# A two-layer transformer with attention and 32 experts on one core: the host lays out every input

## The chip, the cores and the metric

The kernel runs on one core of one Trainium2 chip. The metric is the device time of one execution in microseconds (us), as a median of runs. The engines are TensorE (PE, matrix products; PEld loads its weights), VectorE (DVE), ScalarE (ACT), GpSimd (POOL) and SyncE (SP), which here only issues DMAs. TensorE's clock has two levels, 1.2 and 2.4 GHz; the profile gives the granted clock as a share of the higher one. What the host does with the inputs before the launch is outside the metric.

## The reference

256 tokens with 1024 features go through two layers. Layer 0 has NSA attention (three branches: compressed blocks of keys, selected blocks, a window), layer 1 MoBA attention with keys of its own. After each attention come a mixture of experts (group softmax, then the two best of 8 experts in the token's group) and a gate on a per-layer embedding p. Cut to what matters:

```
for l in (0, 1):
    xn = rms_norm(h, ln_mix[l])
    h  = h + attention_l(xn)                # w_in / w_q, compress_blocks(w1, w2), w_out
    xn = rms_norm(h, ln_ffn[l])
    cw = route(xn @ w_group + b_group, xn @ w_expert + b_expert)        # two experts per token
    h  = h + sum_e cw[:, e] * ((silu(xn @ w_gate[e]) * (xn @ w_up[e])) @ w_down[e])
    h  = h + sigmoid(rms_norm(h, ln_ple[l]) @ ple_w_gate[l]) * (p[l] @ ple_w_proj[l])
```

All inputs and the output are float32; each expert has 1024 x 128, 1024 x 128 and 128 x 1024 weights.

## The kernel before

The residual h stands in SBUF with the token on the partition (two tiles of 128 tokens x 1024 features). A feature product needs the feature on the partition, so `Transposed.fill` (L310) turns h with PE, four 128 x 128 transposes into PSUM, and `split` (L370) cuts the result into a high part (a cast on ACT) and a rest (a subtraction on DVE); three matmuls (L381 to L383: high x high, rest x high or high x rest, and the third) then stand for one product in full precision.

Weights come in through `load`, DMAs on SP's queue into a ring of buffers. `Weights` loads a 1024 x 512 matrix as four tiles of two blocks of 128 rows each (`raw`); `prep` multiplies each block by the norm's gain and splits it: ACT writes the high part (L145), DVE the rest (L146). Where heads are to stand in pairs (`paired`), the high part is L139 and the rest two half operations (L142). `chain` preps three blocks ahead of the one that PE works on. The gains are the columns `g_mix`, made from rows of the norm vectors by a PE transpose (L183) at the start; the other small vectors take a second one (L238).

The head, in its order on PE: L183, 16 transposes of x (L310), four matmuls on ones that compute nothing (`keep_warm`, L177), then the product with the compressed keys' and values' weights (B_c), whose result DVE scales (L331), copies (L651, L652) and adds to positions (L660), then the product with the first selected-branch weights (B_s0), then 32 matmuls with w1 (L702) over which the head norm's matmul L341 is spread.

In attention, `Embedding.turn` (L603 to L608) turns p with four PE transposes and an ACT copy, and L613 uses the result. L485 to L503 turn the softmax's probabilities and multiply them by the values; L472 is a softmax scale on POOL.

The experts of a layer run in eight groups j of four, each with room for 32 tokens, and a ninth short pass for one crowded expert. Before them stands the routing, per half t of the tokens: `logits`, `choose` (DVE, L960 to L970), `order` (PE, L985; DVE, L986) and `place` (DVE, L976), which writes the 0/1 matrix that `gather_first` (PE, L1017) multiplies with h. For that, h is split once more into `h_hi` and `h_lo`: `split_h` on ACT (L995), `rest_h` on DVE (L998). Both read h through `columns(t)` (L289), a view "(p k) -> k p": the feature p*8 + k belongs to block k, so neighbours in a block stand 8 words apart in h. During the experts `unsplit_h` (DVE, L1003) joins the parts to h again through the same view. The four gathers of 128 tokens per group pair alternate between DVE (L1090) and ACT (L1088) after PE's L1064. An expert's gate and up weights come by two DMAs of 512 KB (`load_wgu`, L879 to L888) into one tile; for j = 0 and j = 3 these are large named tiles, of which the fourth (XH in layer 0, XA in layer 1) is the one that holds h, so that its load can be issued only after L998 of the second half has read h.

The order of work on each engine is set by a scheduler that places instructions by their due times when the kernel is built; `tc.issue_after` adds constraints. A DMA on SP can't start before the tile that it writes is free.

## Time and profile before

| | |
|---|---|
| median of 3 runs | 552.87 us (551.81 to 553.31) |
| profiled execution, its own time | 552.15 us |
| its span, first to last instruction | 550.5 us |
| mean granted clock of TensorE | 0.990 |
| PE busy / DVE busy / ACT busy | 523.7 / 351.9 / 282.8 us |
| DMA | 146.14 MB, mean 265 GB/s |

The profiled execution is 0.72 us under the median, and 1.65 us of it lie outside the span. The busy time of an engine overlaps that of the others; what sets the end is read from the waits of the engine that is nearly always busy, and from the instructions around each of them.

### The profile page before, as it was taken

The numbers are of one execution on the slowest core, as the hardware profiler recorded it, in microseconds if no ns is written. First come the engines' busy times: TensorE is split into PE (matmuls) and PEld (weight loads), VectorE is DVE, ScalarE is ACT, GpSimd is POOL, SyncE is SP. The second block draws the span as 40 slices with busy tenths as digits, with TensorE's granted clock in tenths as the row PEclk, the third lists the DMA queues.
The fourth block names the chain that finished last, engine by engine and source line by source line (L and its number), as shares of the span: only waits on it lengthen the run. The fifth ranks groups of instructions, "written<-read, shape, count | busy, mean of one in ns | idle before, by whom it ended". The sixth has DMA issues, their size and how long they took to land. (4 is left out here: it accounts for less than half of the span.)

```text
span 550.5 us, 10449 instructions
## 1 busy us (share of the span) xinstructions
PE 523.7 (95%) x3804; PEld 373.5 (68%) x3804; DVE 351.9 (64%) x1072; ACT 282.8 (51%) x652; POOL 57.9 (11%) x128
## 2 busy tenths in 40 slices
PE   6999999999897999999999999999987999999996
PEld 6979996677567765464568999656556755555376
DVE  5869979988757645323278986767657535232484
ACT  6759468975526142222379956754352412222391
POOL 5000614213320003100000000000000013000000
PEclk9999999999999899999999999999998999999999
DMA  8986980255778499999972679944672999999702
GB/s 324 356 323 223 189 206 1 86 190 205 299 241 302 176 417 408 391 402 409 387 244 78 208 192 216 405 160 199 224 265 106 402 411 413 410 408 395 272 2 77
DMA packets 52940, 146.14 MB, mean 265 GB/s; under 512 B 5293, under 2 KB 10277, under 8 KB 52885
## 3 DMA queue, kind: packets, MB, share of 16 engines
q1 hardware_dynamic: 51669, 143.38, 72.4%
q0 software_dynamic: 1184, 2.05, 1.4%
q8 instruction: 31, 0.51, 0.4%
q14 instruction: 24, 0.20, 0.1%
q10 hardware_dynamic: 32, 0.01, 0.0%
HBM read 145.94 MB, written 1.05 MB: 267 GB/s over the span
## 5 line engine op out<-in xcount | busy, mean ns | idle before, releaser
L1225 PE MATMUL pb<-wgu,X 128*32 128x256 f32 x768 | 50.4, 380 | 1.0 <-DVE sinf L1150 0.4
L461 ACT ACTIVATE p<-p,mx 128x128 f32<-128x128 f32 (+1 forms) x96 | 42.5, 446 | 9.4 <-DVE mx L459 9.4
L865 ACT ACTIVATE p<-pb,srs 128x128 f32<-128x128 f32 x16 | 5.9, 368 | 80.5 <-PE pb L1225 71.0
L1225 PEld LDWEIGHTS pb<-wgu,X 128*32 128x32 f32 x768 | 29.7, 110 | 17.7 <-issue 2.2
L1270 PE MATMUL pb<-wd,hT 128*32 128x512 f32 x224 | 41.4, 596 | 0.0
L370 DVE TENSOR_TENSOR pta<-pb,p 128x512 fp32r<-128x512 f32 (+1 forms) x36 | 24.8, 690 | 24.0 <-ACT p L370 22.5
L370 ACT CAST p<-pb 128x512 fp32r<-128x512 f32 (+1 forms) x36 | 21.1, 585 | 34.7 <-PE pb L1270 33.2
L381 PE MATMUL pa<-XA,wsp 128*128 128x256 f32 x128 | 37.4, 292 | 0.0
L382 PE MATMUL pa<-XB,wsp 128*128 128x256 f32 x128 | 36.3, 284 | 0.0
L383 PE MATMUL pa<-XA,wsp 128*128 128x256 f32 x128 | 35.9, 282 | 0.0
L868 DVE TENSOR_TENSOR p<-pb,ptb 128x128 f32<-128x128 f32 (+1 forms) x18 | 5.2, 290 | 44.1 <-ACT ptb L867 41.8
L459 DVE CUSTOM_DVE_ANT_0 p<-pb,d_q 128x128 f32<-128x128 f32 (+1 forms) x96 | 29.6, 350 | 4.5 <-PE pb L442 3.4
L490 ACT COPY pta<-pa 128x512 f32<-128x512 f32 (+1 forms) x32 | 14.6, 478 | 34.0 <-PE pa L486 33.8
L472 POOL TENSOR_SCALAR p<-p,cf 128x128 f32<-128x128 f32 x32 | 24.8, 783 | 62.8 <-ACT p L461 29.0
L146 DVE SCALAR_TENSOR_TENSOR wsp<-raw,cols,wsp 128x512 fp32r<-128x512 f32 x40 | 28.0, 747 | 3.4 <-ACT wsp L145 3.3
L571 PE MATMUL pa<-wo,XH 128*128 128x512 f32 x64 | 29.4, 602 | 0.0
L1064 PE MATMUL pb<-rs,X 128*128 128x256 f32 (+1 forms) x192 | 27.1, 293 | 2.0 <-DVE X L1090 2.0
L1064 PEld LDWEIGHTS pb<-rs,X 128*128 128x128 f32 x192 | 24.3, 188 | 5.7 <-DVE X L1090 2.6
L1263 PE MATMUL pa<-p,rrow 128*128 128x512 f32 (+1 forms) x72 | 27.3, 424 | 0.0
L1263 PE MATMUL pa<-pta,rrow 128*128 128x512 f32 (+1 forms) x72 | 26.7, 420 | 0.4 <-DVE pta L370 0.4
L142 DVE SCALAR_TENSOR_TENSOR wsp<-raw,g_mix,wsp 128x256 fp32r<-128x256 f32 x64 | 26.5, 475 | 0.0
L145 ACT ACTIVATE wsp<-raw,cols 128x512 fp32r<-128x512 f32 x40 | 26.2, 717 | 0.0
(385 smaller groups left out, 1464.9 us busy)
## 6 DMA issues: line engine op xcount, KB each, us to landing
wgu<-in_moe_w_gate_dram SPq DMA_DIRECT2D x48, 512.0 KB, 6.5
wgu<-in_moe_w_up_dram SPq DMA_DIRECT2D x48, 512.0 KB, 10.2
wd<-in_moe_w_down_dram SPq DMA_DIRECT2D x48, 512.0 KB, 8.8
raw<-in_a_w_in_dram SPq DMA_DIRECT2D x16, 512.0 KB, 6.0
raw<-in_ple_w_gate_dram SPq DMA_DIRECT2D x16, 512.0 KB, 8.3
wd<-in_moe_w_down_dram SPq DMA_DIRECT2D x16, 256.0 KB, 6.2
wo<-in_a_w_out_dram SPq DMA_DIRECT2D x8, 512.0 KB, 8.4
raw<-in_b_w_q_dram SPq DMA_DIRECT2D x8, 512.0 KB, 4.4
```

What stands on the lines that cost most here:

```text
L146: nc.vector.scalar_tensor_tensor(lo, src, g, hi.bitcast(F32), ALU.mult, ALU.subtract)
L370: return nc.scalar.copy(hi, src), eng.tensor_tensor(lo, src, hi.bitcast(F32), ALU.subtract)
L381: nc.tensor.matmul(o, a[0], b[0], start=first, stop=False)
L382: nc.tensor.matmul(o, a[0], b[1], start=False, stop=False)
L383: return nc.tensor.matmul(o, a[1], b[0], start=False, stop=last)
L459: nc.vector.tensor_tensor_reduce(pt_[:, br, :], st_[:, br, :], dt_, -SLOPE[hh], 3e38, ALU.add, ALU.min, accum_out=mx[:, t, br:br + 1])
L461: mark["exp", c] = nc.scalar.activation(pt_[:, br, :], pt_[:, br, :], AF.Exp, bias=mx[:, t, br:br + 1], scale=-1.0, accum_out=sums[:, t, b ...
L571: m = nc.tensor.matmul(pt, self.oT[0][:, 2 * j + i, t * P:(t + 1) * P], self.raw[j][:, i, n * 512:(n + 1) * 512], start=(i == 0), stop=(i ...
L1064: nc.tensor.matmul(pt, part_columns(x, t)[:, k, :], Gs[i][:, t, 0:e1], start=(t == x == 0), stop=(t == x == 1))
L1225: last_ = nc.tensor.matmul(gu[32 * i:32 * i + 32, 0:2], xg[:, k, 32 * i:32 * i + 32], wgu[i][k], start=(k == 0), stop=(k == NK - 1), tile_ ...
L1263: nc.tensor.matmul(y[t][n], gt[0:m, t * P:(t + 1) * P], ysx[x][0:m], start=(first and x == 0), stop=(final and x == 1))
L1270: nc.tensor.matmul(ysp[32 * i:32 * i + 32, :], hT[:, 32 * i:32 * i + 32], wd[i][n], start=True, stop=True, tile_position=(0, 32 * i))
```

## The change

The host hands the inputs over in the shape in which SBUF holds them. (1) x comes also turned (`xT`); `cut` splits it straight from SBUF, interleaved with B_c's preps, and the 16 transposes go. x itself is loaded behind B_c's weights, 1 MB more in all. (2) All norm vectors and positions come as one table of columns, `vec`, by one DMA on ACT's queue with 312 bytes per partition; ten small DMAs, two PE transposes and their copies go. (3) `keep_warm` runs eight matmuls at PE's very start. (4) p comes turned; `turn` goes. (5) Projection weights lie in blocks, in pairs of heads where that is wanted: one contiguous run per partition in each DMA (4 KB instead of two of 2 KB; w1 16 KB instead of 16 runs of 1 KB; w_out, gate and up 8 KB), and one L131 in place of two L142. (6) Gate and up of one expert come by one DMA of 1 MB. (7) The experts' weights, the router and its gain stand in h's own order, "(k p)", so that a block of h is 128 neighbouring words. (8) The fourth tile of j = 0 moves to the ring; the late one is now used by j = 1. Line numbers below are those of the kernel after.

```diff
-                self.raw.append(load([P, 2, self.n], lambda t: [(t, wrows(w, c0, c1)[:, k:k + 2])], "raw"))
-                if small:
-                    nc.sync.dma_start(*small.pop(0))
+                if turned is not None:
+                    xT.append(load([P, 2, S], lambda t: [(t, turned[:, k:k + 2])], "xT"))
+                self.raw.append(load([P, 2, self.n], lambda t: [(t, w[:, k:k + 2])], "raw"))
...
-                    for b in range(2):
-                        o = pairs(lo)[:, :, b, :]
-                        nc.vector.scalar_tensor_tensor(o, src[:, b * 256:(b + 1) * 256].rearrange("p (i d) -> p i d", d=HD),
-                                                       g, pairs(hi)[:, :, b, :].bitcast(F32), ALU.mult, ALU.subtract)
+                nc.scalar.activation(hi, src, AF.Copy, scale=g)
+                nc.vector.scalar_tensor_tensor(lo, src, g, hi.bitcast(F32), ALU.mult, ALU.subtract)
...
+    vec = cp.tile([P, 78], F32, name="vec")
+    nc.scalar.dma_start(vec, I["vec"])
+    g_mix = vec[:, 0:16].rearrange("p (l k) -> p l k", l=2)
+    B_c = Weights(I["w_c"], g_mix[:, 0, :], I["xT"])
+    nc.sync.dma_start(hh[0], I["x"][0].rearrange("(t p) d -> p t d", p=P))
+    B_s = [Weights(I["w_s0"], g_mix[:, 0, :])]
...
-        return hh[0][:, t, :].rearrange("q (p k) -> q k p", k=NK)
+        return hh[0][:, t, :].rearrange("q (k p) -> q k p", k=NK)
...
-        def turn(self):
-            self.pT = ring.tile([P, 2, S], F32, name=nm("pT"))
...
-            nc.scalar.copy(self.pT, pt)
+            self.pT = load([P, 2, S], lambda t: [(t, I["pT"][l])], "pT")
...
-    for t in range(NT):
-        for n in range(2):
-            f_ = X.fill(t, n)
+    for k in range(0, NK, 2):
+        f_ = X.cut(k, xT.pop(0))
+        B_c.prep(k + 2)
...
-    with tc.issue_after(X.last.ins):
-        keep_warm(pts[0], 4)
+    keep_warm(pts[0], 8)
...
-                if j in (0, 3):
+                if j == 3 or (j == 0 and i < 3) or (j == 1 and i == 3):
...
-                for x in range(2):
-                    nc.sync.dma_start(w[:, x], gu[x])
+                nc.sync.dma_start(w, I["moe_gu"][l, e])
```

What the scheduler makes of it stands here at three places. The first is VectorE in the head: the rests of B_s0's weights (L146 before, L131 after, one per `wsp`), the scaling of B_c's result (L331 before, L301 after), and its copies and sums (L651, L652, L660 before; L605, L606, L614 after). Before:

```order
L146 SCALAR_TENSOR_TENSOR wsp_467<-raw_99,g_mix,wsp_467 128x512
L331 TENSOR_TENSOR p_45_391<-pa_277,rrow_265 128x512
L331 TENSOR_TENSOR p_46_400<-pa_278,rrow_265 128x512
L651 COPY X_37_274<-p_45_391 64x2x256
L652 COPY X_37_274<-p_45_391 64x2x255
L651 COPY X_37_274<-p_46_400 64x2x256
L660 TENSOR_TENSOR X_38_275<-X_37_274,cols 128x512
L660 TENSOR_TENSOR X_38_275<-X_37_274,cols 128x32x15
L652 COPY X_37_274<-p_46_400 64x2x255
L146 SCALAR_TENSOR_TENSOR wsp_482<-raw_102,g_mix,wsp_482 128x512
```

After:

```order
L131 SCALAR_TENSOR_TENSOR wsp_363<-raw_97,vec,wsp_363 128x512
L301 TENSOR_TENSOR p_42_366<-pa_248,rrow_239 128x512
L301 TENSOR_TENSOR p_43_375<-pa_249,rrow_239 128x512
L605 COPY X_34_245<-p_42_366 64x2x256
L606 COPY X_34_245<-p_42_366 64x2x255
L605 COPY X_34_245<-p_43_375 64x2x256
L614 TENSOR_TENSOR X_35_246<-X_34_245,vec 128x512
L614 TENSOR_TENSOR X_35_246<-X_34_245,vec 128x32x15
L606 COPY X_34_245<-p_43_375 64x2x255
L131 SCALAR_TENSOR_TENSOR wsp_427<-raw_99,vec,wsp_427 128x512
L614 TENSOR_TENSOR X_35_246<-X_34_245,vec 128x512
L614 TENSOR_TENSOR X_35_246<-X_34_245,vec 128x32x15
```

Before, `wsp_467` is the sixth of B_s0's eight blocks, and two are left behind the scaling; after, `wsp_363` is the fourth, and four are left, the fifth (`wsp_427`) in front of the second pair of sums and the sixth to eighth behind it.

The second is TensorE after B_s0's last product: the matmuls with w1 (L702 before, L656 after) and the head norm's sum of squares (L341 before, L311 after). Before, the seven rows that follow the product are matmuls with w1, and then:

```order
L702 MATMUL pa_568<-a_cv_w_52_415,X_38_275 64x256
L702 MATMUL pa_568<-a_ck_w_51_413,X_38_275 64x256
L341 MATMUL pb_552<-sq_550,blk_119 128x512
L702 MATMUL pa_568<-a_cv_w_52_415,X_38_275 64x256
L702 MATMUL pa_568<-a_ck_w_51_413,X_38_275 64x256
```

After, from the product's last rows on:

```order
L352 MATMUL pa_402<-wsp_472,XA_188 128x256
L353 MATMUL pa_402<-wsp_472,XB_189 128x256
L656 MATMUL pa_543<-a_ck_w_48_388,X_35_246 64x256
L311 MATMUL pb_527<-sq_525,blk_114 128x512
L656 MATMUL pa_543<-a_cv_w_49_390,X_35_246 64x256
```

Seven matmuls with w1 stood ahead of the sum of squares, and now one.

The third is VectorE in the routing of layer 0, after the choice of experts for the first half of the tokens: the rest of h (L998 before, L951 after), the second half's logits (L954; L907), the rank (L986; L939) and its place (L976; L929). Before:

```order
L968 TENSOR_TENSOR A_376_2074<-iota_e,ei_2072 128x64
L954 SCALAR_TENSOR_TENSOR lg_2065<-pa_2164,rstd_2064,rb 128x36
L970 TENSOR_TENSOR A_2075<-A_376_2074 128x32
L998 TENSOR_TENSOR X_380_2078<-XH_75,X_379_2077 128x1024
L986 SCALAR_TENSOR_TENSOR rank_2076<-pa_2179,A_2075 128x32
```

After:

```order
L921 TENSOR_TENSOR A_371_2018<-iota_e,ei_2016 128x64
L923 TENSOR_TENSOR A_2019<-A_371_2018 128x32
L951 TENSOR_TENSOR X_375_2022<-XH_75,X_374_2021 128x1024
L907 SCALAR_TENSOR_TENSOR lg_2009<-pa_2108,rstd_2008,rb 128x36
L939 SCALAR_TENSOR_TENSOR rank_2020<-pa_2123,A_2019 128x32
```

The second half's logits stood ahead of the rest of h, and now stand behind it.

## Rows read from the trace of the kernel before

**Rows 1.** Section 1 of the page: engine, busy us, share of the span, instructions.

```profile
PE 523.7 (95%) x3804; PEld 373.5 (68%) x3804; DVE 351.9 (64%) x1072; ACT 282.8 (51%) x652; POOL 57.9 (11%) x128
```

**Rows 2.** Waits of the matmul engine: engine, line <- releaser: us in total, times, longest us.

```profile
PE pb L1017 <- DVE rs L976: 4.7, 2, 2.5
...
PE pb L183 <- POOL islp L206: 3.8, 1, 3.8
...
PE pb L1064 <- DVE X L1090: 2.0, 3, 0.8
...
PE pa L485 <- POOL p L472: 1.6, 1, 1.6
...
PE pb L1225 <- DMA XA<-in_moe_w_up_dram: 1.5, 1, 1.5
...
PE pb L1147 <- DVE X L1090: 0.9, 2, 0.5
```

**Rows 3.** Timeline of the head: start us, us, engine line op out<-in, [idle before <-releaser].

```profile
4.47 3.68 PE L310 MATMUL pb<-ident,XH 128*128 128x128 f32 x16 [0.43 <-DMA XH<-in_x_dram]
...
8.19 0.59 ACT L370 CAST XA<-pb 128x512 fp32r<-128x512 f32 x1 [0.27 <-PE pb L310]
...
9.45 0.62 PE L381 MATMUL pa<-XA,wsp 128*128 128x256 f32 x1
...
21.45 1.39 DVE L331 TENSOR_TENSOR p<-pa,rrow 128x512 f32<-128x512 f32 x2
...
26.39 0.75 DVE L146 SCALAR_TENSOR_TENSOR wsp<-raw,g_mix,wsp 128x512 fp32r<-128x512 f32 x1
...
28.92 0.75 DVE L146 SCALAR_TENSOR_TENSOR wsp<-raw,g_mix,wsp 128x512 fp32r<-128x512 f32 x1
...
32.82 0.69 DVE L331 TENSOR_TENSOR rs<-pa,rrow 128x512 f32<-128x512 f32 x1 [3.15 <-PE pa L383]
```

**Rows 4.** Table by stretches: stretch, us, busy us of each engine, PEclk, DMA share, GB/s.

```profile
4.00:6.00 2.00, 1.56 (x8) 1.53 (x8) 0.17 (x1) 0.37 (x1) 1.42 (x21) 1.00 0.99 395
...
20.00:22.00 2.00, 2.00 (x19) 2.00 (x19) 2.00 (x5) 1.49 (x3) 0.00 (x0) 1.00 1.10 347
```

**Rows 5.** Timeline of the routing, layer 0 (three rows), then layer 1 (last row).

```profile
173.29 1.98 DVE L998 TENSOR_TENSOR X<-XH,X 128x1024 fp32r<-128x1024 f32 x1
...
175.90 1.22 PE L1017 MATMUL pb<-rs,X 128*128 128x256 f32 x8 [2.47 <-DVE rs L976]
...
180.36 3.75 PE L1017 MATMUL pb<-rs,X 128*128 128x256 f32 x16 [0.72 <-DVE es L1112]
...
417.76 2.13 PE L1017 MATMUL pb<-rs,X 128*128 128x256 f32 x16 [0.71 <-DVE es L1112]
```

**Rows 6.** Table by stretches, the end of the routing of layer 0.

```profile
176.00:184.40 8.40, 7.37 (x40) 6.68 (x43) 7.04 (x34) 2.80 (x6) 0.62 (x3) 0.59 0.49 184
```

**Rows 7.** Timeline of the attention of layer 0, the turning of p.

```profile
90.46 0.66 PE L607 MATMUL pa<-ident,pr 128*128 128x128 f32 x4
...
91.94 1.13 PE L613 MATMUL pa<-wp,pT 128*128 128x512 f32 x2 [0.82 <-ACT pT L608]
```

**Rows 8.** Timeline of the experts of layer 0, the joining of h.

```profile
217.88 2.14 DVE L1003 TENSOR_TENSOR XA<-X,X 128x1024 f32<-128x1024 f32 x1
```

**Rows 9.** Groups of instructions, shapes kept apart: count | busy us, mean ns of one.

```profile
L381 PE MATMUL pa<-XA,wsp 128*128 128x256 f32 x128 | 37.4, 292 | 0.0
...
L295 ACT ACTIVATE sq<-XH 128x1024 bf16<-128x1024 f32 x6 | 6.3, 1052 | 3.1 <-DVE XH L574 3.1
...
L995 ACT CAST X<-XH 128x1024 fp32r<-128x1024 f32 x2 | 4.2, 2084 | 0.0
...
L998 DVE TENSOR_TENSOR X<-XH,X 128x1024 fp32r<-128x1024 f32 x2 | 4.0, 2014 | 0.0
```

**Rows 10.** Table by stretches, the experts of layer 0.

```profile
188.00:262.00 74.00, 71.83 (x670) 41.15 (x670) 29.74 (x102) 19.76 (x48) 7.42 (x8) 1.00 1.01 398
```

**Rows 11.** DMA issues: tensor, queue, count, KB each, median us from issue to landing.

```profile
p<-in_a_ck_w_dram POOLq DMA_DIRECT2D x1, 64.0 KB, 5.4
```

More of the change, by code (lines that the diff above doesn't have):

```diff
@@ L179, in keep_warm @@
         return i
-    pt = pb([P, 16])
-    nc.tensor.transpose(pt, rows[0:16], ident[0:16, 0:16])
-    nc.vector.tensor_copy(g_mix.rearrange("p l k -> p (l k)"), pt)
     ones_r = cp.tile([P, P], F32R, name="ones_r")
@@ L228, in hybrid_kernel @@
     bm = cp.tile([P, 2], F32, name="bm")
-    cols = cp.tile([P, 62], F32, name="cols")
+    cols = vec[:, 16:78]
     pos, hg = cols[:, 0:32], cols[:, 32:38]
@@ L234, in hybrid_kernel, with query_gains @@
     qg = [cp.tile([P, 8], F32, name=f"qg{l}") for l in range(2)]
[L236 to L239 removed]
+    def query_gains():
         for l in range(2):
@@ L311, in fill, with cut @@
             return split(*[v[:, 4 * n:4 * n + 4, t * P:(t + 1) * P] for v in self.x], pt)
+        def cut(self, k, raw):
+            return split(*[v[:, k:k + 2] for v in self.x], raw)
         def norms(self):
@@ L551, in hybrid_kernel, with __init__ @@
     class Out:
-        def __init__(self, w, oT, l):
+        def __init__(self, oT, l):
             self.oT, self.w, self.raw, self.add_at, self.l = oT, {}, [], ADD_AT[l], l
             for j in range(4):
-                a, i0 = divmod(2 * j, 4)
-                r0 = a * 512 + i0 * HD
-                self.raw.append(load([P, 2, D], lambda t: [
-                    (t[b * HD:(b + 1) * HD], w[r0 + b * 256:r0 + b * 256 + 2 * HD, :]
-                     .rearrange("(i j) n -> j i n", j=HD)) for b in range(2)], "wo"))
+                self.raw.append(load([P, 2, D], lambda t: [(t, I["w_out"][l, j])], "wo"))
         def add(self, j, t, n):
@@ L626, in hybrid_kernel @@
     X = Transposed("XA", "XB")
-    for t in range(NT):
-        for n in range(2):
-            f_ = X.fill(t, n)
+    for k in range(0, NK, 2):
+        f_ = X.cut(k, xT.pop(0))
+        B_c.prep(k + 2)
     with tc.issue_after(f_[0].ins):
-        B_c.prep(NK)
         X.norms()
@@ L714, in hybrid_kernel @@
     nc.vector.tensor_tensor(hx, hx, hu, ALU.mult)
-    B_q = [Weights(w_in, a * 512, (a + 1) * 512, gm0, True) for a in range(2)]
+    B_q = [Weights(I["a_q"][a], gm0) for a in range(2)]
     kv_branch(1, lambda: B_q[0].prep(4))
@@ L1163, in moe, with rows_of @@
         srsx = st("srsx", [CAP, 1], bufs=1)
-        def rows_of(src, o):
-            rows = I[src].rearrange("l e d f -> (l e d f)").rearrange("(r n) -> r n", n=D)
+        def rows_of(rows, o):
             nc.gpsimd.memset(o, 0.0)
@@ L1384, in load_ple @@
     def load_ple(l):
-        return [Weights(I["ple_w_gate"][l], n * 512, (n + 1) * 512, g_ple[:, l, :]) for n in range(2)]
+        return [Weights(I["ple_gate"][l, n], g_ple[:, l, :]) for n in range(2)]
     def ple(B, X, nxt=None):
@@ L1428, in hybrid_kernel @@
     gm1 = g_mix[:, 1, :]
[L1429 removed]
+    B_kv = Weights(I["w_kv"], g_kv)
     dump("h2", hh[0])
@@ L1452, in use_kv @@
             X.norms()
-            B_q.extend(Weights(I["b_w_q"][0], a * 512, (a + 1) * 512, gm1, True) for a in range(2))
+            B_q.extend(Weights(I["b_q"][a], gm1) for a in range(2))
         if k == NK - 1:
@@ L1508 @@
     arrays, aps = {}, {}
-    for name in _INS:
-        a = _np.ascontiguousarray(inputs[name])
+    for name, a in _layout(inputs).items():
         arrays[f"in_{name}_dram"] = a
```

108 lines of the change are left out of this document (50 added, 58 removed).

## The prediction

> **What bounds the kernel now.** I read the busy times first. PE is busy 523.7 us, 95% of the span, and DVE and ACT far less [rows 1]; so a change can save at most what PE waits, plus the PE work that it takes out, plus time that PE spends at its lower clock. The change takes out little PE work, so I went next to the list of PE's waits [rows 2]: 4.7 us in two waits for the matrix of places (L1017), 3.8 at the start, 2.0 and 0.9 for DVE's L1090 in the experts, 1.6 for a softmax step on POOL, 1.5 for one expert tile's DMA. Then I read the timeline around each of them, and last the clock. All sums are made against the profiled execution (552.15 us, span 550.5); the median is 0.72 us above it, and I take the saving off the median.
>
> **The head.** Before, x lands, PE turns it from 4.47 us on in 16 transposes, ACT and DVE split it, and the product with B_c starts at 9.45 [rows 3]. After, PE does nothing that counts until the first quarter of xT and the first two blocks of weights are there. 512 KB had landed by 4.47; 0.75 MB and the table are some 300 KB more, 0.7 us at the 395 GB/s of 4-KB rows [rows 4], so 5.2; one cast of the kind that took 0.59 [rows 3] hides the second half of that transfer, another like it makes the first block: the product starts at about 5.8, 3.65 us earlier. The transfers of all 3 MB allow that (2.6 MB after 4.47 at 395 GB/s end at 11.1, and a quarter of the 12.0 us product is left then). But the first matmul of the product took 0.62 us where the mean of its kind is 0.292 [rows 3, 9]: PE begins at its lower clock, and the earlier it begins the longer it stays there. Bounds for the product's end are 0 and 3.65 us earlier; I take 2.0.
>
> Little of that arrives. In the new order DVE has four of B_s0's eight blocks, not two, behind the scaling of B_c's result. Counted from the start of that scaling (21.45), the first rest behind it was done at 27.14, 5.7 us later, and the second at 29.67, 8.2 us later [rows 3]. One block occupies PE for (32.82 - 21.45) / 8 = 1.42 us, so the fifth block is wanted after 5.7 us, just met, and the sixth after 7.1, met 1.1 us late; the last two follow at 0.75 each and are in time. So 1.1 lost, with bounds of 0 (before, these slots held blocks that PE wanted later) and 2.5 (the fifth late by as much). Then the head norm: its chain behind the product is a scaling of 0.69 and a square on ACT, as long as a cast, 0.59 [rows 3]; seven matmuls with w1 covered it, and in the new order one does. I take 0.9 lost (bounds 0, and 1.9 with a second ACT step ahead of it). **Head: 2.0 - 1.1 - 0.9 = 0**, between -4.4 and +3.65.
>
> The other edits of the head cost nothing: x itself comes 1 MB later, but the norms that read it come behind ACT's preps of B_c in both orders, and w1 gives the time back (it moved at 347 GB/s in 1-KB runs, 4-KB rows at 395 [rows 4]: 4 MB, 1.4 us of queue). If that cover went, 1 MB at 395 GB/s is 2.7 us. One L131 for two L142 frees DVE in attention, where PE's list has no wait for these weights.
>
> **Attention.** Four transposes and the wait behind them stand between 90.46 and 91.94 on PE; 0.82 of it is the wait for ACT's copy [rows 7], and the transposes are 0.66 with overlap. That is at most 1.5 in layer 0. In layer 1 only the transposes count, 0.6. What follows is a softmax chain through ACT, DVE and POOL, with a wait of its own of 1.6 for L472 [rows 2], which can take the gift back. Bounds 0 and 2.1; I take **1.6**, near the top, since the waits named in this stretch are few.
>
> **Routing.** ACT's split of h takes 2.08 us and DVE's rest 2.01, each over 1024 elements through the 8-word stride; a contiguous 1024 on ACT takes 1.05, and a contiguous 512 on DVE 0.69 [rows 3, 9]. Twice 0.69 is 1.38, and one start is paid once, so my estimate is 1.27: 0.73 saved (0.62 to 0.9). DVE's rest of h stands directly before rank and place, for which PE waits 2.47 us [rows 5]. The new order also puts the second half's logits behind it, and fills with the rest a stretch in which DVE waited for them: 0.25 more in layer 0. For the second half, the rest stands again before rank and place, and the wait of 0.72 (layer 1: 0.71) [rows 5] falls by 0.7. Sum: 0.73 + 0.25 + 0.72 in layer 0, 0.73 + 0.71 in layer 1, **3.15** (bounds 2 and 4.4, where ACT's shorter split helps too). Late next is PE's own queue of gathers, and at the first wait still this chain.
>
> **The late tile.** The 1.5 us wait for XA's second DMA [rows 2] stands in layer 1, at the first group's fourth expert. In the new order this tile is in the ring, and the one that waits for h serves the second group, a whole group later. **1.5**, to 0 if the ring has no room in time.
>
> **Joining h.** L1003 takes 2.14 us, twice per layer [rows 8]; by the same estimate 1.27, so 0.87 less each. It stands on DVE ahead of L1090, for which PE waits 2.0 and 0.9 in all, single waits up to 0.8 and 0.5 [rows 2]. Each of the four waits behind an L1003 is under the 0.87 that is saved. Together 2.0 + 0.9, less the 0.4 of one L1090 wait elsewhere; **2.2**, with 1.0 and 2.5 as bounds, as one small DVE step is still between.
>
> **The clock.** From 176.0 to 184.4 the granted clock averaged 0.59 [rows 6]. It fell after the two waits of 2.47 and 0.72, and 16 gathers took 3.75 us there, where the same 16 in layer 1 took 2.13 [rows 5], so 1.6 us were lost. With shorter waits it may fall later or not at all, or just as before: **0.5**, bounds -0.8 and 1.6.
>
> **Sum:** 0 + 1.6 + 3.15 + 1.5 + 2.2 + 0.5 = 8.95 us; 552.87 - 8.95 = **543.9**.
>
> **Rivals.** (A) Half of it is taken back. The attention's gift ends at the softmax step of L472, the clock falls as before, and the joining saves 1.0: 3.15 + 1.5 + 1.0 = 5.65, less 1.1 for a head that starts late: 548.3. For it: PE's stretches in attention are tied to ACT and DVE by many short waits. Against: in routing and experts the releasing step itself gets shorter. 0.18.
>
> (B) The head keeps its 3.65 or most of it, as DVE has its rests ready earlier throughout, and the clock stays up: 8.95 + 2.9 + 1.1 = 12.95, so 539.9. For it: DVE's first rests begin some 3 us earlier too. Against: the order of rows. 0.12.
>
> (C) The table is late. The nearest rows are 64 KB in 256-byte pieces, 5.4 us to landing [rows 11]. Issued at about 0.9 us it would come at 6.3, and the first block, which is multiplied by it, at 6.9: 1.1 of the head's 2.0 goes, 545.0. The Trainium skill, DMA: Bandwidth & Descriptors, Specifications, says that a transfer needs 512 bytes or more for line rate, and that below it the engine reads, modifies and writes; the table's 312 bytes are below. No run here shows such a table yet. 0.08.
>
> (D) The stride isn't what makes these operations slow (the type that they write, or their length, could be): then routing, joining and clock keep their times, and 8.95 - 5.85 = 3.1 remain: 549.8. For it: no contiguous twin of L998 stands in the trace. Against: on ACT a contiguous 1024 takes half [rows 9]. The Trainium skill, Vector Engine (DVE) Microarchitecture Reference, Measured stream behaviour on trn2, has a rule that bears on this: a port streams at full rate only over pairs of adjacent words, and one source that hops at every element makes 1.73 ns of 1.054. By it, L998 would fall by 0.69 us to 1.32, and the sum would be 8.8; the trace's 2.01 against the 1.27 that I estimate stands in nearly the same ratio. 0.06.
>
> (E) Slower than before: the transfers become the bound of the experts. In 188 to 262 us they run at 398 GB/s beside 71.83 us of PE work in 74 [rows 10]: 29.5 MB, with hardly any room. If one DMA of 1 MB in 8-KB pieces ran only as fast as the slowest saturated stretch, 347 GB/s [rows 4], the same bytes would take 85 us, 11 more per layer, of which half may be hidden by the lead of the loads: 543.9 + 11 = 555. It decides below 398 GB/s. Against it: rows of 4 KB did better than rows of 1 KB, so longer ones should not do worse. The Trainium skill, DMA: Bandwidth & Descriptors, Specifications, with line rate from 512 bytes up, would give relaid weights the same rate as before; the trace differs for 1-KB runs (347 against 395 [rows 4]), and neither points to a loss. 0.06.
>
> **How the numbers follow.** Forecast 0.50 (543.9), A 0.18, B 0.12, C 0.08, D 0.06, E 0.06. The range reaches to A and C, past D's edge and to B: 539.5 to 549.8; E and the tails of B and D are left out. A difference of 0.3%, 1.7 us, is about what can be told from none here. All but E and half of D lie more than that below 552.87: faster 0.91, same 0.03, slower 0.06.
>
> **What would show it.** In the profile after: the splits of h at about 1.05 (ACT) and 1.27 (DVE); the wait for the matrix of places at 1.5 to 1.8 twice instead of 2.5 and 2.2; no wait for XA; the L1090 waits nearly gone; no wait at the gate's product with p; in the head a product start near 5.8, a wait for a DVE rest of B_s0 near its sixth block, and one of about 0.9 at the sum of squares. Wrong it would be if DVE's 1024 stays at 2 us, if a DMA stands among PE's waits in the experts, or if the time before the first expert shrinks by less than 3 us or by more than 9.

## The result and the profile after

Measured side by side, the kernel after takes 546.21 us (median of 4 runs), the kernel before 552.34 (551.67 to 553.31). One of the four runs was disturbed (554.82), and the ratio goes by the three others, 544.41 to 546.59: it is 0.9872, with an interval of [0.9853, 0.9891], or 7.1 us. The forecast was 543.9 in a range of 539.5 to 549.8: direction and range held, and the gain was 6.1 us by the medians, 7.1 by the ratio, for a forecast 8.95. The profiled execution took 546.59, with a span of 544.8, 5.7 less than before.

Section 1 of the page after (engine, busy us, share, instructions), which answers to [rows 1]:

```profile
PE 518.6 (95%) x3782; PEld 364.3 (67%) x3782; DVE 341.0 (63%) x1038; ACT 278.7 (51%) x650; POOL 51.9 (10%) x120
```

PE's busy time fell by 5.1 us; its idle time hardly moved, 550.5 - 523.7 = 26.8 before and 544.8 - 518.6 = 26.2 after. So waits went and others came. PE's list of waits after (engine, line <- releaser: us in total, times, longest us) answers to [rows 2]:

```profile
PE pa L351 <- ACT wsp L130: 4.1, 2, 3.3
PE pb L970 <- DVE rs L929: 3.1, 2, 1.6
PE pa L353 <- DVE wsp L131: 2.0, 2, 1.2
PE pb L1183 <- DMA X<-in_moe_gu_dram,rowi: 1.8, 1, 1.8
...
PE pa L351 <- DVE rs L301: 0.7, 1, 0.7
...
PE pb L311 <- ACT sq L309: 0.6, 1, 0.6
...
PE pb L692 <- DVE p L78: 0.4, 1, 0.4
```

Gone are the waits for p's turning, for POOL's softmax step and for the late tile; of those for DVE's step L1090 (L1043 after) in the experts, 2.9 us before, 0.3 is left. The wait for the matrix of places (L929) is shorter. New are five in the head (L130, L131, L301, L309, L78) and one for a gathered transfer in layer 1 (L1183).

To place the gain I read the starts of the same instructions in PE's timelines of both kernels. The table gives how far the kernel after is ahead at each point (minus: behind), and what the stretch up to it brought:

| point on PE | before | after | ahead | stretch | forecast |
|---|---|---|---|---|---|
| first turning of probabilities, layer 0 | 86.93 | 91.57 | -4.63 | head -4.6 | 0 |
| product with p, layer 0 | 91.94 | 95.10 | -3.16 | p +1.5 | 1.6 with the next row and layer 1 |
| last of attention, layer 0 | 173.22 | 175.46 | -2.24 | +0.9 | |
| experts j = 0 end, layer 0 | 188.20 | 187.50 | +0.71 | routing, clock +2.95 | 3.65 with layer 1 |
| experts j = 4 start, layer 0 | 223.41 | 221.14 | +2.28 | joining h +1.6 | 2.2 with layer 1 |
| gate/up of the last group end, layer 0 | 269.34 | 266.74 | +2.60 | +0.3 | |
| last result of the experts, layer 0 | 281.32 | 281.31 | +0.01 | last group -2.6 | none |
| logits, layer 1 | 405.38 | 405.13 | +0.25 | +0.2 | |
| experts j = 0 start, layer 1 | 419.82 | 417.80 | +2.02 | routing, clock +1.8 | (above) |
| experts j = 0 end, layer 1 | 425.61 | 421.46 | +4.15 | late tile +2.1 | 1.5 |
| experts j = 4 start, layer 1 | 460.77 | 455.18 | +5.59 | joining h +1.4 | (above) |
| experts j = 5 start, layer 1 | 473.65 | 469.87 | +3.78 | ninth pass -1.8 | none |
| end | 550.45 | 544.76 | +5.69 | rest, last group +1.9 | |

By these stretches, every part that was forecast as a gain brought what was forecast or more, 12.5 us against 8.95: attention 2.6, routing and clock 4.7, tile 2.1, joining 3.0. Within a stretch it came partly by other ways than forecast, as shown below. The head, forecast at 0, lost 4.6, and two stretches that the forecast did not name lost 4.4; small change and layer 1's last group gave 2.2.

**The head.** Its timeline after (start us, us, engine line op, [idle before <- releaser]) answers to [rows 3]:

```profile
5.08 0.62 ACT L340 CAST XA<-xT 128x512 fp32r<-128x512 f32 x1 [2.98 <-DMA xT<-in_xT_dram]
7.23 1.33 ACT L130 ACTIVATE wsp<-raw,vec 128x512 fp32r<-128x512 f32 x2 [1.53 <-DMA raw<-in_w_c_dram]
8.00 0.58 PE L351 MATMUL pa<-XA,wsp 128*128 128x256 f32 x1 [3.26 <-ACT wsp L130]
...
13.08 0.41 PE L353 MATMUL pa<-XA,wsp 128*128 128x256 f32 x1
...
13.48 0.28 PE L352 MATMUL pa<-XB,wsp 128*128 128x256 f32 x1
...
15.92 1.06 ACT L261 ACTIVATE sq<-XH 128x1024 bf16<-128x1024 f32 x1 [1.13 <-DMA XH<-in_x_dram]
...
19.89 0.28 DVE L292 TENSOR_SCALAR hT<-ident,rstd 128x128 f32<-128x128 f32 x1
...
22.62 0.38 PE L293 MATMUL pb<-hT,ones_r 128*128 128x128 f32 x2
23.04 0.37 ACT L295 COPY rrow<-pb 128x256 f32<-128x256 f32 x1 [1.92 <-PE pb L293]
23.45 1.29 DVE L301 TENSOR_TENSOR p<-pa,rrow 128x512 f32<-128x512 f32 x2 [1.29 <-ACT rrow L295]
...
29.82 0.39 PE L353 MATMUL pa<-XA,wsp 128*128 128x256 f32 x1 [1.20 <-DVE wsp L131]
32.34 0.38 PE L353 MATMUL pa<-XA,wsp 128*128 128x256 f32 x1 [0.82 <-DVE wsp L131]
37.54 1.12 PE L311 MATMUL pb<-sq,blk 128*128 128x512 f32 x2 [0.57 <-ACT sq L309]
```

xT came about when it was expected (5.08). But the first block of weights landed only at 7.2, and the product began at 8.00, not 5.8. Its matmuls then took 0.41 us until 13.3 and 0.28 from there on; before, they were at 0.28 from 10.43, one us into the product. I read these as the lower and the higher level of the clock from the matmuls' own times, because the granted clock in this trace's rows stands at 1.00 all along; the traces of `gather_order` and `h_strided`, whose first matmuls go at about this pace, give 0.50 from 8 to 10 us. Some 4.3 us more at the slower pace cost 2.2, more than the 1.45 won at the start.

The scaling came at 23.45 instead of 21.45. It waits for ACT's copy of the norm (L295), which waits for the turning of the norm on PE (L293). That stands behind the whole product, its second step at 22.62. Before, it stood inside the product:

```profile
18.05 0.38 PE L323 MATMUL pb<-hT,ones_r 128*128 128x128 f32 x2
```

The norm itself (hT, DVE L292) was ready by 20.2, while PE was still busy with the product. So it is the order that the scheduler gave PE that made the scaling late, and not x's landing.

Behind the scaling stand the two waits for rests of B_s0 (1.2 and 0.8; 1.1 was forecast) and the one at the sum of squares (0.6; 0.9 was forecast). The loss now adds up. The first matmul with w1 is 2.9 us later than before (36.33 for 33.43): 1.45 won at the start, 2.2 lost by the pace, 2.0 in the two waits. With the 0.6 at the sum of squares and two waits further on that the trace of before does not have (0.7 for L301, 0.4 for L78), it is 4.6.

The table by stretches (columns as in [rows 4]; last column GB/s) shows how slowly the first transfers moved; before, 4 to 6 us stood at 395, but 2 to 4 us at 272:

```profile
2.00:4.00 2.00, 2.00 (x6) 0.73 (x5) 0.00 (x0) 0.10 (x1) 1.62 (x13) 1.00 0.83 189
4.00:6.00 2.00, 0.74 (x2) 0.00 (x0) 0.28 (x1) 0.62 (x1) 1.41 (x21) 1.00 0.87 239
```

**h.** The groups of the three operations that now read or write h contiguously (columns as in [rows 9]), in place of 2084, 2014 and 2140 ns:

```profile
L948 ACT CAST X<-XH 128x1024 fp32r<-128x1024 f32 x2 | 2.1, 1040 | 0.0
...
L956 DVE TENSOR_TENSOR XH<-X,X 128x1024 f32<-128x1024 f32 x2 | 2.4, 1222 | 3.3 <-PE pb L1177 3.3
...
L951 DVE TENSOR_TENSOR X<-XH,X 128x1024 fp32r<-128x1024 f32 x2 | 2.4, 1217 | 0.0
```

The forecast said 1.05 and 1.27. The Trainium skill, Vector Engine (DVE) Microarchitecture Reference, Measured stream behaviour on trn2, gives 1.73 against 1.054 ns per element for one source that hops by 4 KiB at every element, a ratio of 1.64. Here the step is only 8 words, and the ratio in the traces is about the same, 2014 / 1217 = 1.65.

**Routing and clock.** Timeline of the routing of layer 0, PE and one row of DVE, as in [rows 5], then the tables of that stretch (as [rows 6]) and of the experts (as [rows 10]):

```profile
177.17 2.01 PE L970 MATMUL pb<-rs,X 128*128 128x256 f32 x8 [1.51 <-DVE rs L929]
...
181.10 0.19 DVE L1091 COPY cnt<-pa 128x32 f32<-128x32 f32 x1 [0.88 <-PE pa L1090]
...
181.77 2.13 PE L970 MATMUL pb<-rs,X 128*128 128x256 f32 x16 [0.71 <-DVE es L1065]
```

```profile
176.00:184.40 8.40, 6.52 (x49) 6.01 (x53) 7.35 (x40) 3.00 (x7) 0.62 (x3) 0.80 0.74 263
...
188.00:262.00 74.00, 73.09 (x673) 41.67 (x672) 29.43 (x104) 20.80 (x49) 6.27 (x6) 1.00 1.01 410
```

The first wait fell from 2.47 to 1.51. The second stayed at 0.71, where the forecast had taken off 0.7 in each layer: DVE was done with the rest of h at 180.05, but then waited 0.88 for PE's count of tokens (L1090), which is queued behind the first half's gathers, and the places (L929) stand behind that copy. In its place came the clock: it fell as before, after the first wait, but was up again in time for the last sixteen gathers, 2.13 instead of 3.75. The first sixteen were slower than before by 0.6, so that layer 0's 32 gathers took 6.0 us instead of 7.0. In layer 1 the first wait fell from 2.24 to 1.59, the second did not fall either (0.71 and 0.77), and the first sixteen gathers took 2.4 instead of 3.8. So of the 4.7 us of both layers the shorter waits gave 1.6 and the faster gathers 2.4. The transfers of the experts ran at 410 GB/s, not slower than 398: rival E is out.

**What nobody had named.** In layer 0 the products with `w_down` of the last group stand in another order. First the kernel before, then the one after, on PE:

```profile
276.18 1.92 PE L1270 MATMUL pb<-wd,hT 128*32 128x512 f32 x14
```

```profile
273.69 1.90 PE L1221 MATMUL pb<-wd,hT 128*32 128x512 f32 x10
275.52 0.74 PE L1214 MATMUL pa<-p,rrow 128*128 128x512 f32 x2
276.19 1.05 PE L1221 MATMUL pb<-wd,hT 128*32 128x512 f32 x2
277.17 0.74 PE L1214 MATMUL pa<-pta,rrow 128*128 128x512 f32 x2
277.84 1.04 PE L1221 MATMUL pb<-wd,hT 128*32 128x512 f32 x2
```

Each of these matmuls uses 32 of PE's 128 columns, and sixteen make up the group. In the trace of before one pair stands apart from them, in that of after three do, two of them behind the scatter (L1214). A pair alone takes 1.04 to 1.05 us; a row of 4, of 10 or of 14 takes 1.90 to 1.92, so a row's time does not follow its count. Two pairs more cost about 2.1 us. In layer 1 it is the other way round: before had the cut order, after has the whole one.

The ninth pass gathers the weights of the crowded expert by POOL. Before, gate and up went first and down last; after, down (XB) goes first, and the large gather behind it:

```profile
450.35 1.74 POOL L1120 DMA_INDIRECT XB<-in_moe_w_down_dram,rowi  x1 [0.16 <-POOL X L1119]
452.40 0.99 POOL L1120 DMA_INDIRECT X<-in_moe_gu_dram,rowi  x1 [0.30 <-issue]
...
465.13 0.59 PE L1183 MATMUL pb<-X,ptb 128*32 128x256 f32 x2 [1.78 <-DMA X<-in_moe_gu_dram,rowi]
```

### The profile page after: what moved, and what is told of

Read it like the earlier page. It is cut to its first block, busy times and chain, and to the rows that moved or that the text cites. A ratio compares the mean times of both kernels' runs of the same rounds, so it can differ in the third digit from the quotient of the medians.

```text
span 544.8 us, 10203 instructions
## 1 busy us (share of the span) xinstructions
PE 518.6 (95%) x3782; PEld 364.3 (67%) x3782; DVE 341.0 (63%) x1038; ACT 278.7 (51%) x650; POOL 51.9 (10%) x120
## 3 DMA queue, kind: packets, MB, share of 16 engines
HBM read 146.98 MB, written 1.05 MB: 272 GB/s over the span
## 5 line engine op out<-in xcount | busy, mean ns | idle before, releaser
L131 DVE SCALAR_TENSOR_TENSOR wsp<-raw,vec,wsp 128x512 fp32r<-128x512 f32 (+1 forms) x96 | 67.4, 747 | 5.5 <-ACT wsp L130 5.3
L130 ACT ACTIVATE wsp<-raw,vec 128x512 fp32r<-128x512 f32 (+1 forms) x96 | 62.6, 719 | 2.8 <-DMA raw<-in_w_c_dram 2.1
L1177 PE MATMUL pb<-wgu,X 128*32 128x256 f32 x768 | 56.9, 381 | 0.9 <-PEq L1295 0.6
L351 PE MATMUL pa<-XA,wsp 128*128 128x256 f32 x128 | 38.3, 299 | 4.0 <-ACT wsp L130 3.3
L353 PE MATMUL pa<-XA,wsp 128*128 128x256 f32 x128 | 37.2, 292 | 2.0 <-DVE wsp L131 2.0
L460 ACT COPY pta<-pa 128x512 f32<-128x512 f32 (+1 forms) x32 | 14.6, 479 | 32.4 <-PE pa L456 32.4
L351 PEld LDWEIGHTS pa<-XA,wsp 128*128 128x128 f32 x128 | 25.3, 198 | 5.9 <-ACT wsp L130 4.2
L1214 PE MATMUL pa<-p,rrow 128*128 128x512 f32 (+1 forms) x72 | 27.1, 424 | 0.2 <-ACT p L340 0.2
L353 PEld LDWEIGHTS pa<-XA,wsp 128*128 128x128 f32 x128 | 25.1, 197 | 2.4 <-DVE wsp L131 2.4
```

Source lines behind the costliest of these rows:

```text
L130: nc.scalar.activation(hi, src, AF.Copy, scale=g)
L131: nc.vector.scalar_tensor_tensor(lo, src, g, hi.bitcast(F32), ALU.mult, ALU.subtract)
L351: nc.tensor.matmul(o, a[0], b[0], start=first, stop=False)
L353: return nc.tensor.matmul(o, a[1], b[0], start=False, stop=last)
L1177: last_ = nc.tensor.matmul(gu[32 * i:32 * i + 32, 0:2], xg[:, k, 32 * i:32 * i + 32], wgu[i][k], start=(k == 0), stop=(k == NK - 1), tile_ ...
L1214: nc.tensor.matmul(y[t][n], gt[0:m, t * P:(t + 1) * P], ysx[x][0:m], start=(first and x == 0), stop=(final and x == 1))
```

## The experiments

The theory by now: contiguous h pays as forecast, the late tile and p too; the head costs 4 us, first of all because its first transfers are slow; and the scheduler took back another 4 by two orders that nobody asked for. The rivals: the table is late (C); the stride is not the cause (D); one of the orders follows from the projection weights' preps.

**The head taken back** (x loaded first and turned by PE as before, everything else as after):

```diff
-    B_c = Weights(I["w_c"], g_mix[:, 0, :], I["xT"])
-    nc.sync.dma_start(hh[0], I["x"][0].rearrange("(t p) d -> p t d", p=P))
+    B_c = Weights(I["w_c"], g_mix[:, 0, :])
...
-    for k in range(0, NK, 2):
-        f_ = X.cut(k, xT.pop(0))
-        B_c.prep(k + 2)
+    for t in range(NT):
+        for n in range(2):
+            f_ = X.fill(t, n)
```

> The kernel after, with the head of before: x is loaded first and turned by PE, its splits follow, the eight preps of B_c come behind them, four matmuls on ones behind the transposes; the table of vectors and the weights by blocks stay. In the trace of after, the attention's first transposes start 4.6 us later than before. If that is lost for good, this kernel is 4 to 5 us faster than after, about 541.6. The rival: what the head gains or loses is taken up by the waits of the softmax chain and the late loads, and the time stays at 545 to 546.

Measured: 542.47 us (541.76 to 545.87), ratio 0.9827 [0.9795, 0.986], span 540.7. Its first attention turning starts at 86.88, as before, and the lead stays to the end: 9.8 us in spans against 5.7, although PE has a stall of 2.1 here that it does not have in after (see the end). So the new head costs some 4 us in the profiled executions. By the ratios it is 2.5, and their intervals overlap slightly; the size is not settled by the times.

**Contiguous blocks for the first transfers.** In the kernel after, each DMA of w_c takes 4 KB out of every 16 KB of host memory, and each of xT 2 KB out of 8. Here each DMA's data lie in one piece:

```diff
-                    xT.append(load([P, 2, S], lambda t: [(t, turned[:, k:k + 2])], "xT"))
-                self.raw.append(load([P, 2, self.n], lambda t: [(t, w[:, k:k + 2])], "raw"))
+                    xT.append(load([P, 2, S], lambda t: [(t, turned[k // 2])], "xT"))
+                self.raw.append(load([P, 2, self.n], lambda t: [(t, w[:, k:k + 2] if turned is None else w[k // 2])], "raw"))
```

> The kernel after, with xT and B_c's weights stored so that each of their eight DMAs reads one contiguous piece of HBM (before that, each partition's 4-KB run lay 16 KB from the next). In after, B_c's first 4-KB packets take 290 ns where 160 is usual, and the first product waits until 8.0 us. If the pitch of the source makes the first transfers slow, they run at about 400 GB/s from 3 us on, the product starts at about 6, and the time falls by 1 to 2 us. If it is the table of vectors or the start of the transfers as such, the product still starts at 8.0 and the time stays within 0.5 us of 546.2.

Measured: 548.09 us (545.2 to 552.43), 0.9924 [0.9867, 0.998], span 543.4. The time decides nothing; the trace does. The head's timeline and stretches of this kernel:

```profile
4.18 0.62 ACT L340 CAST XA<-xT 128x512 fp32r<-128x512 f32 x1 [2.08 <-DMA xT<-in_xT_dram]
5.43 1.34 ACT L130 ACTIVATE wsp<-raw,vec 128x512 fp32r<-128x512 f32 x2 [0.63 <-DMA raw<-in_w_c_dram]
6.20 0.39 PE L351 MATMUL pa<-XA,wsp 128*128 128x256 f32 x1 [1.47 <-ACT wsp L130]
6.43 0.28 PE L352 MATMUL pa<-XB,wsp 128*128 128x256 f32 x1
...
26.66 0.39 PE L353 MATMUL pa<-XA,wsp 128*128 128x256 f32 x1 [1.42 <-DVE wsp L131]
```

```profile
2.00:4.00 2.00, 2.00 (x6) 0.71 (x5) 0.00 (x0) 0.10 (x1) 1.62 (x13) 1.00 0.89 293
4.00:6.00 2.00, 0.73 (x2) 0.00 (x0) 0.69 (x1) 1.19 (x2) 1.40 (x21) 1.00 0.90 320
```

The same bytes by the same DMAs came at 293 and 320 GB/s instead of 189 and 239, and the product began at 6.20. That the place of the runs in memory made the first transfers slower is shown, in one profiled execution each. It is not all of it, for in one piece too they stay under the 395 that the prediction took, and from 8 to 10 us the kernel after moved the same kind of runs at 416. Why the first microseconds are slow stays open. The product went at its full pace from the second matmul on, so that the first matmul with w1 starts at 33.17, 3.2 us ahead of after: 1.8 from the start and most of the rest from the pace. The three waits behind the scaling stay (1.4, 0.8, 0.6), and the first attention turning is still 1.6 us behind before.

**The table widened** to 512 bytes per partition:

```diff
-    vec = cp.tile([P, 78], F32, name="vec")
+    vec = cp.tile([P, 128], F32, name="vec")
```

> The kernel after, with the table of vectors widened from 78 to 128 columns by zeros, so that its runs are 512 bytes instead of 312. If runs under 512 bytes make the table late or hold up the transfers beside it, the first product starts before 7 us instead of at 8.0 and the time falls by about 1 us. The rival: the table had landed long before the first weights, and nothing changes (8.0 us, 546.2).

Measured: 547.52 us (546.81 to 551.08), 0.992 [0.9885, 0.9954]. The table landed 4.4 us after its issue in both kernels, and the product began at 8.07 instead of 8.00. Rival C is out: the table was not what the first block waited for. The Trainium skill (DMA: Bandwidth & Descriptors, Specifications) gives 512 bytes as the least size for line rate. For this one small transfer the traces show no difference between 312 and 512 bytes.

**h with its stride back** (features in the old order "(p k)", weights, router and gain with them, everything else as after):

```diff
-        return hh[0][:, t, :].rearrange("q (k p) -> q k p", k=NK)
+        return hh[0][:, t, :].rearrange("q (p k) -> q k p", k=NK)
```

> The kernel after, with one part undone: the experts' weights, the router and its gain again in the order (p k), so that the views of h step 8 words; all else stays. If the stride is what made the splits slow and they stood in PE's way, the splits of h go back from 1.2 to 2.0 us and the joins to 2.1, and the time rises by about 5.9 us (3.15 routing, 2.2 joining, 0.5 clock) from 546.2 to about 552. If the stride only made them busy beside other work, it rises by less than 2 us.

Measured: 556.69 us (555.02 to 558.3), 1.0072 [1.0046, 1.0099], slower than before. From its groups and PE's waits:

```profile
L951 DVE TENSOR_TENSOR X<-XH,X 128x1024 fp32r<-128x1024 f32 x2 | 4.0, 2012 | 0.0
```

```profile
PE pb L970 <- DVE rs L929: 4.7, 2, 2.5
...
PE pb L1177 <- issue: 2.6, 1, 2.6
PE pb L1017 <- DVE X L1043: 2.0, 3, 0.8
...
PE pb L1100 <- DVE X L1043: 0.8, 2, 0.5
```

The durations and the waits are back to what they were before, so rival D is out. But the step is worth 10.5 us between the medians (8.4 between the profiled spans), not 5.85. In the trace, 4.1 us are these waits, 2.6 a stall at the last group that only some kernels have (see the end), and the granted clock was at its lower level, 1.2 GHz, for 13.7 us in the two routings, against 3.4 after: up to 5.1 us.

**Contiguous h alone**, put into the kernel before (the view of h as in the kernel after, and the host's order of the experts' weights, router and gain):

```diff
-        return hh[0][:, t, :].rearrange("q (p k) -> q k p", k=NK)
+        return hh[0][:, t, :].rearrange("q (k p) -> q k p", k=NK)
```

> The kernel before, with one part of the change alone: the experts' and the router's feature rows are handed over in the other order, and the view of h reads 128 neighbouring words per block. If the routing and the joining of h return what their shorter steps promise wherever they stand, the time falls by 5.9 us at least (3.15 routing, 2.2 joining, 0.5 clock), to about 546.9, and by up to 8 if the half-speed stretch of the clock in the routing ends with it (8.4 us lay between the spans when the same part was undone in the kernel after). The rival: part of that was a wait of 2.6 us elsewhere that the undone kernel happened to have, and the part alone is worth 5 us or less.

Measured: 545.5 us (545.14 to 548.22), 0.9868 [0.985, 0.9886]. One edit out of eight gives the whole gain of the change. The other seven together are worth nothing that can be measured: what they brought, the head and the two orders took. The forecast for this step, routing, joining and clock, was 5.85; 7.0 was measured. It has a part more: PE's wait of 1.5 for the late tile is gone here too, although the tile was not moved. Its DMA, which waits for h to be read, is issued at 413.13 instead of 417.10. So the 2.1 us of the tile's stretch are not shown to come from moving the tile.

**The fourth tile of j = 0 late again:**

```diff
-                if j == 3 or (j == 0 and i < 3) or (j == 1 and i == 3):
+                if j in (0, 3):
```

> The kernel after, with the fourth tile of the first group again the late one. If the wait of before (1.5 us in layer 1) was that tile's, PE waits for its DMA again at the first group of layer 1, 1.5 us or more, as h is now read faster but the load is one of 1 MB and not two, and the time rises by 1.5 us to about 547.7. If the shorter routing alone had taken the wait away, nothing changes.

Measured: 555.31 us (553.35 to 558.38, nine runs), 1.0045 [1.0026, 1.0065]: 9 us, six times what was expected. PE's waits, and the stretches behind them:

```profile
PE pb L1177 <- issue: 2.6, 1, 2.6
PE pb L1177 <- DMA XH<-in_moe_gu_dram: 2.3, 1, 2.3
```

```profile
186.00:188.00 2.00, 2.00 (x28) 1.09 (x24) 0.00 (x0) 0.00 (x0) 0.00 (x0) 0.62 0.02 8
...
270.00:275.50 5.50, 3.31 (x26) 1.35 (x28) 0.29 (x1) 0.96 (x3) 0.00 (x0) 0.69 1.02 407
...
420.00:428.60 8.60, 7.44 (x44) 6.82 (x48) 6.71 (x38) 2.96 (x7) 0.54 (x2) 0.62 0.51 194
```

The forecast was a wait of 1.5 or more in layer 1. The tile's own wait is 2.3 us, and it stands in layer 0: its DMA of 1 MB is issued at 180.22, as soon as h has been read, and lands 5.5 us later, while the faster routing wants it at 183.5. Before, there were two DMAs of half the size and a slower routing, and no wait here; which of the two hid it was not tried. Since h is read contiguously here, the tile in its old place can cost PE a wait even so. After this wait the clock fell within the full product, where half speed is paid in full, and again after the stall of 2.6 and in the routing of layer 1. In this execution, 12 us slower than after, the wait is 2.3, the stall 2.6, and most of the rest lies in stretches at the lower level. That the other runs have the same split is not shown: their mean clocks are 0.983 to 0.995, and their times do not follow them. How 2.3 become 9 in the median stays open.

**The order of the last group.** First a rival: the preps of the gate's weights ahead of the turning of h, as before (layer 0's loss would follow from it).

```diff
+            if n == 0:
+                later[0].prep(3)
             for t in range(NT):
                 X.fill(t, n)
-            if n == 0:
-                later[0].prep(3)
```

> The kernel after, with the gate's first weight preps written ahead of the turning of h instead of behind it; all else stays. In the trace of after, the 2.6 us that layer 0 is ahead of before at its last expert are gone at its end: ACT does two casts for h before the first prep, and PE waits 0.9 us for that prep. If that order is the cause, layer 0 keeps 1 to 2.6 us more and the time falls to about 544.5. If PE waits for something else there (the transfers of the gate's weights, the sum of h), it stays at 546.2.

Measured: 552.13 us in ten runs from 544.72 to 554.27, 0.996 [0.9924, 0.9997]. The time is unclear. In the trace (span 544.6) the last result of layer 0 comes where it came after, so it is not the cause. Then the products themselves, held together by letting the final scatter be issued only behind the last of them:

```diff
+            with ExitStack() as es:
+                if final:
+                    es.enter_context(tc.issue_after(d_.ins))
+                for n in range(2):
+                    for t in range(NT):
+                        scatter(t, n, ysxs[n])
```

> The kernel after, with one constraint more: in the last group of experts the products that add to the tokens come behind all eight of its down products. In after, the scheduler puts three of these eight one by one between other work in layer 0 (and keeps them together in layer 1; before it is the other way round), and the 2.6 us that layer 0 is ahead at its last gate product are gone after its last down product. If single down products are the cause (about 1 us each, where four together take 1.9), layer 0 keeps 2 us more and the span falls from 544.8 to about 542.7. If it is the weights of the gate behind them, the span stays at 544.8.

Measured: 544.2 us (543.69 to 544.85), 0.9842 [0.9826, 0.9858], span 543.0. The row on PE is whole again:

```profile
275.82 1.92 PE L1221 MATMUL pb<-wd,hT 128*32 128x512 f32 x14
```

From the end of gate and up to the last result, layer 0 takes 12.1 us, as before (12.0), where after took 14.6. So the order is shown as the cause of that loss. Between the ratios it is 0.3%, 1.7 us; in the profiled execution the clock was low from 176 to 186 us, 10 us instead of 3.4, which takes back part.

**The order of the gathers:** gate and up first, down behind.

```diff
+            g_ = rows_of(I["moe_gu"].rearrange("l e p x k f -> (l e p) (x k f)"), wx[0].rearrange("p x d -> p (x d)"))
...
+            with tc.issue_after(g_.ins):
+                rows_of(I["moe_w_down"].rearrange("l e f d -> (l e f) d"), wx[1])
```

> The kernel after, with the rows of the crowded expert gathered in the other order: gate and up first, then down. In after, down's gather was issued first, and in layer 1 PE waited 1.8 us for gate and up, which landed 12.7 us after their issue. If the order is the cause, that wait goes and the time falls by 1 to 1.8 us, to about 544.8. If the one gather of 1 MB is late because it shares the engines with the 1-MB loads of the next group, the wait stays above 1 us.

Measured: 545.95 us (543.35 to 548.83), 0.9893 [0.986, 0.9927], span 541.5. The large gather is issued 3.6 us sooner (1.2 of it because PE is that much further by then), and no wait for it is left in PE's list:

```profile
448.79 1.02 POOL L1120 DMA_INDIRECT X<-in_moe_gu_dram,rowi  x1 [0.27 <-DVE X L1043]
```

The mechanism is shown in the trace; between the medians it is lost in the spread.

**Together.** Three versions: the head of before, w_c in contiguous blocks and the gathers' order;

> The kernel after with three edits: the head of before (x first, turned by PE), B_c's weights stored so that each of their DMAs reads one contiguous piece, and the crowded expert's gate and up gathered before its down rows. The head of before alone gave 542.5. If the gather's order matters as in the other run, about 541.3; B_c's pieces should be worth nothing here, as the product waits for PE's transposes. The rival: the reordering by the scheduler costs what the gather saves, 542.5 again.

544.16 us (543.68 to 545.97), 0.985 [0.9824, 0.9877], with a stall of 2.3 at the last group of layer 1. The 541.3 that was expected did not come, and the head of before alone, with a stall of 2.1, gave 542.47; the two intervals overlap. Then the head of before with both orders;

> Three edits to the kernel after: the head of before (x first, turned by PE), the crowded expert's gate and up gathered first, and the last group's down products kept together in both layers. The head of before alone gave 542.5; the other two should be worth 1 to 1.8 and 2 us: about 539.5. If the three take each other's gain back, or PE's sequencer stops for 2 us in the last group of layer 1 as it did in two kernels with this head, 541 to 542.

540.63 us (539.92 to 542.14), 0.979 [0.9768, 0.9811], span 537.9: faster than both kernels. And the new head with contiguous blocks and six of B_s0's blocks ahead of the scaling, with both orders:

> Four edits to the kernel after, with its own head: xT and B_c's weights in contiguous pieces, six of B_s0's blocks prepared ahead of the scaling instead of four, the gather's order, and the last group's down products kept together. The pieces gave 1.8 us at the product's start; the two waits of 1.2 and 0.8 for B_s0's rests should go, so that the products with w1 begin at about 31 instead of 36.3, and the time is about 538. If x's late landing sets the scaling and so the rests, they begin at 33 and the time is 540 to 541.

543.21 us (542.43 to 543.86), 0.983 [0.9813, 0.9848], span 540.9. Its product starts at 6.32 and the first matmul with w1 1.4 us ahead of before, but it reaches the first attention turning at 87.57, 0.6 behind; a wait of 1.4 for a square on ACT (at 56.2 us) took most of that. The interval lies apart from that of the kernel with the old head, but that is not the head's doing alone: that kernel reaches this turning at 87.06, so of the 3.0 us between the spans the head has 0.5, and most of the rest is a stall of 2.6 in layer 0's last group here (that kernel's own, 2.0, stands in layer 1). With these mends the head without transposes is about as fast as the one with them, and no faster.

## Why the prediction was right, and where it was not

**The head (0, measured -4.6)** is the step that failed. The prediction let the product end 2.0 us earlier, from a start 3.65 earlier. The start came 1.45 earlier, and the slower pace at its begin cost 2.2, so the product ended later and not earlier. The start was priced at 395 GB/s, from the stretch of 4 to 6 us, in which x's second half and B_c moved; the stretch just before it in the same trace had 272, and the first transfers of the new kernel moved at 189 and 239. "The earlier it begins the longer it stays there" named the pace without giving it a price of its own. The -1.1 and -0.9 behind it were right in kind (2.0 and 0.6), but two later waits of 0.7 and 0.4 for DVE were not in the sum. The bound of 4.4 lost at worst was just too small.

**x itself later costs nothing:** ACT waited 1.13 for it, but no wait of PE is shown to come from it. What the sentence did not see is that the turning of the norm could move behind the product, which made the scaling 2.0 us late.

**Attention (1.6, measured 2.6)** was right for layer 0, with 1.5 in the stretch with p; layer 1 brought 0.2 where 0.6 was forecast. POOL's softmax step, for which PE waited 1.6 in layer 0's attention before, did not take it back; that wait is gone, while waits for ACT's copies there grew from 0.7 to 1.9. Why was not tried, so the cause of the 0.9 behind p's stretch stays open.

**Routing (3.15) and clock (0.5)** hold in sum (4.7 for 3.65), not in parts. The durations were right to 0.05 us, and the first wait fell by 1.0 in layer 0 and by 0.65 in layer 1. The second wait did not fall at all, so the waits gave 1.6 of 3.15. The prediction had said what would be late next, PE's own queue of gathers, and had not let it hold here: the count behind them kept DVE waiting. The gathers themselves, by whose time the clock was priced, ran faster by 2.4 for a forecast 0.5, 1.0 in layer 0 and 1.4 in layer 1. That the sum came out near is in part luck.

**Joining (2.2, measured 3.0)** was right as a mechanism. **The late tile (1.5, measured 2.1)** was right in that the wait went; but contiguous h alone took it away too, so moving the tile is not shown to be the cause.

**Not named:** two orders that the scheduler changed on the way, -2.6 (with +1.3 given back in layer 1) and -1.8. Both stood in the order of the instructions, where I had looked only at the engines that a term rested on. Two of the signs of being wrong came true with the head and these orders: a DMA stands among PE's waits in the experts (L1183), and by the end of layer 0's first group PE was only 0.7 us ahead, where less than 3 before the first expert was to be a sign.

Of the rivals, C's time (545.0) lies nearest to the result, then A's (548.3) and the forecast's own (543.9), about equally far. C's mechanism is out, and so is A's but for its late head: neither attention nor joining gave anything back. What took the gain was a slow head, for another reason than C's, and two lost orders.

## What to carry to other kernels

Where an engine reads or writes through a stride, have the host lay the data out so that it is contiguous: one edit here was worth 1.3%. Removing work from the start is not the same as starting sooner: price the first transfers by the first microseconds and by where their runs lie in memory, and what stands behind them by the order of the instructions on every engine that it passes. After any edit that moves a scheduler, compare its order of the groups that it did not mean to touch.

## What the hardware showed that I had not expected

- The same bytes in the same DMAs came at 189 and 239 GB/s when each took 4 KB out of every 16 (2 out of 8) of host-laid memory, and at 293 and 320 from one piece, from 2 to 6 us into the kernel.
- A pair of matmuls that use 32 columns of PE took 1.04 us where it stood alone, and a row of 4, 10 or 14 of them took 1.90 to 1.92.
- At the last group's gate and up, PE stood 2.0 to 2.6 us with no releaser that the profile shows ("issue"), in six of the kernels tried and not in the rest, in one layer each. What causes it was not tried.
- The stretches at the lower clock come after waits of PE, but not after each: in layer 0's routing two of the kernels (`best1f`, `gather_order`) have none. They last from 3.4 to 10.2 us from kernel to kernel. Contiguous h alone had two of 10.2 in its profiled run, with a span of 546.5, and no such mean clock in its four others, which were 2.4 to 3.1 us faster.
